# Pinning weight transfers, activation-sum transfers and a norm scaling to program order in the down stage

## The chip, the cores and the metric

The kernel is one program on one core of a Trainium2 chip. The metric is the device time of one execution in microseconds (us), and less is better. Before the change three runs took 1169.48, 1171.72 and 1176.24 us; the median is 1171.72 us. The profiled execution is a fourth one, with a time of its own.

## The reference, cut to what matters

One decoder layer over 16 meta tokens and 256 sequence tokens, model width 2048. Two groups of heads (differential attention and retention) share an input projection and an output projection; a gated MLP of width 5632 with a causal convolution over three tokens follows, and then a final RMS norm. Everything is float32.

```python
u = rmsnorm(h, attn_norm[l]) * vmask
proj = u @ w_in[l]
...
y = jnp.concatenate([ya.reshape(B, L, D_A), yr.reshape(B, L, D_R)], axis=-1)
h = h + y @ w_out[l]
u = rmsnorm(h, ffn_norm[l]) * vmask
h = h + conv_glu(u, w_gate[l], w_up[l], conv_w[l], w_down[l])
out = rmsnorm(h, final_norm)

def conv_glu(u, w_gate, w_up, conv_w, w_down):
    g = u @ w_gate
    gc = ...                      # three-tap causal convolution of g
    return (jax.nn.silu(gc) * (u @ w_up)) @ w_down
```

The change touches the last product, `@ w_down`, a 256 x 5632 by 5632 x 2048 product, and the multiplication by `final_norm` behind it.

## The kernel before, in words

**Splitting.** A float32 operand is carried as two parts, a rounded "hi" part and the remainder "lo", and a product is three matmuls: hi by hi, hi by lo and lo by hi. So each piece of weights that arrives in SBUF is prepared twice before TensorE can use it: ScalarE (ACT) casts it into a tile `whi` (L180), and VectorE (DVE) subtracts that from the original into `wlo` (L181). There are three `whi` and three `wlo` buffers, so a cast waits until TensorE has finished with the piece three places earlier.

**Stages.** Input projection and heads, output projection, gate and up products (44 blocks `f`, L740 on), then the down stage, which starts about 924 us into the span and ends with the output. Weights stream in from HBM as chunks of 128 x 2048 floats (1 MB), one DMA each (L162), issued by SyncE (SP) on one queue. A chunk goes into one of three buffers with the tag `raw`. SP issues in its order and waits, at each DMA, until that DMA's buffer is free; whatever stands behind it on SP waits too.

**The down stage.** Output columns are handled in two groups `g` of 1024. Of the 44 blocks of 128 MLP channels, the first 16 are multiplied in eight pairs by a scheme that needs seven block products where four 2 x 2 blocks would need eight. Its weights are the eight "mixed" chunks of a group (`in_w_mix_dram`), and it uses sums of activations as well as the activations. Those sums were made in the gate and up stage and stored in DRAM tiles `sd`; in the down stage they come back as eight transfers of 512 KB into the two tiles `sf` (L159). A mixed chunk is worked in four parts, `b`, `d`, `u` and `t`, each of which needs an addition or subtraction on DVE besides the cast and the `wlo` (L188 to L196). The other 28 blocks are plain chunks (`in_w_down_dram`), of which each gives two entries of twelve matmuls. `down_order` writes the sequence: in group 0, six plain entries lead, and then the parts of the mixed chunks and the rest of the plain entries alternate; group 1 begins with a mixed chunk.

**Buffers that matter here.** A mixed chunk of even number goes into a buffer of its own, `sraw` in the pool `dn`; the odd ones use `raw`. `dn` stands where the pool of the gate and up stage (`fw`) stood, so `sraw` is free only once the last gate and up block has been finished on DVE (L763, `flo`). The two `sf` tiles stand where the gate and up stage's input stood, and each is free once TensorE has read its half for the last time.

**The final norm's vector.** Half of it at a time is broadcast into the tile `fn` by a DMA that GpSimd (POOL) issues (L792, `norm`), and DVE multiplies it by -0.5 (L797, `norm_scale`). It is used by `weigh` (L836), after a group's sums have been added up. The program text puts `norm_scale` twelve empty steps of the side list behind `norm`.

**What sets the order.** The kernel is written as one stream of instructions. A scheduler that has a time model of its own then decides, for each engine, the order in which the instructions stand; it keeps dependencies, and not the order of the text. In the text, `load` issues a mixed chunk's `sf` transfer immediately ahead of the chunk itself. The call `tc.keep_in_program_order(ins)` adds an edge of order (no wait) from the instruction that stands before `ins` on the same engine in the text.

Of the kernel before, what the change touches and what calls it, by code (L numbers as in the profile page):

```python
# [10 lines left out]
F32 = mybir.dt.float32  # L11
# [4 lines left out]
ALU = mybir.AluOpType  # L16
# [67 lines left out]
def down_order():  # L84


    out = []
    for g in range(2):
        plain = [("w", 2 * g + j, b) for j in range(2) for b in range(NPL)]
        parts = [("s", p, q) for p in range(NS) for q in PARTS]  # L90
        lead, tail = LEAD[g]
        mid = plain[lead:len(plain) - tail]
        seq = plain[:lead]
        done = 0
        for i, part in enumerate(parts):
            seq.append(part)
            to = (i + 1) * len(mid) // len(parts)
            seq += mid[done:to]
            done = to
        out.append(seq + plain[len(plain) - tail:])  # L100
    return out
# [3 lines left out]
def trunk_kernel(ctx, tc, a, out):  # L105
    nc = tc.nc
    V, S, PE = nc.vector, nc.scalar, nc.tensor
# [10 lines left out]
    chunks = []  # L118
# [6 lines left out]
    for j in range(NF):  # L125
        chunks.append(a["w_gate"][j])
        chunks.append(a["w_up"][j])
    entries = [(c, h) for c in range(len(chunks)) for h in range(2)]
    order = down_order()
    mixed = {}  # L130
# [15 lines left out]
    pools = {}  # L146
# [5 lines left out]
    def load(c):  # L152
        if c in mixed and mixed[c] % 2 == 0:
            t = pools["dn"].tile([P, D], F32, tag="sraw", name=f"raw{c}")
        else:
            t = wp.tile([P, D], F32, tag="raw", bufs=3, name=f"raw{c}")
        if mixed.get(c, NS) < NS:
            p = mixed[c]
            nc.sync.dma_start(  # L159
                out=pools["sf"][p // (NS // 2)][:, p % (NS // 2)].rearrange(  # L160
                    "p a b c -> p (a b c)").bitcast(F32), in_=pools["sd"][p])
        nc.sync.dma_start(out=t, in_=chunks[c])  # L162
        raw[c] = t

    def prep(hf):
# [41 lines left out]
    def ahead(hf):  # L207
        while state["dma"] < len(chunks) and opens[state["dma"]] <= hf + 4:
            load(state["dma"])
            state["dma"] += 1  # L210
        while state["prep"] < len(entries) and state["prep"] <= hf + 2:
            prep(state["prep"])
            state["prep"] += 1
# [49 lines left out]
    with tc.tile_pool(name="start", bufs=2) as st:  # L263
        acc = st.tile([P, 4, T], F32, name="acc", bufs=1)
        xrs, rws = [], []
        for c in range(4):
# [6 lines left out]
            for b, e in cuts:  # L273
                lead = c == 0 and b == 0
                (nc.scalar if lead else nc.sync).dma_start(
                    out=xr[:, b:e], in_=a["x"][:, 4 * c + b:4 * c + e])
# [5 lines left out]
        for c in range(4):  # L282
            xr, rw = xrs[c], rws[c]
            for half in range(2):
                whi = wp.tile([P, 1024], F32R, tag="whi", bufs=3, name=f"whi{2 * c + half}")
                wlo = wp.tile([P, 1024], F32R, tag="wlo", bufs=3, name=f"wlo{2 * c + half}")
                for jj in range(2):
# [6 lines left out]
                                           op0=ALU.mult, op1=ALU.subtract)  # L294
# [9 lines left out]
                    for t, (t0, n) in enumerate(FN):  # L304
                        b = jj * 512 + t * P
# [131 lines left out]
    with ExitStack() as p1:  # L437
# [203 lines left out]
        for h in range(AH):  # L641
# [6 lines left out]
                                   op0=ALU.mult, op1=ALU.mult)  # L648
# [20 lines left out]
        for kind, r in RSEQ:  # L669
            if kind == "g":  # L670
                for c in range(2):
                    g = ap_.tile([P, TV], F32, tag=f"g{c}", name=f"rg{r}_{c}")[:, :NQ]
# [28 lines left out]
        for j in range(KT):  # L701
# [15 lines left out]
            for i in range(4):  # L717
                c = j * P + i * 32
                nc.sync.dma_start(
                    out=hd[:, c:c + 32].rearrange("(b t) f -> t b f", t=32),  # L720
                    in_=hb[i * 32:(i + 1) * 32].rearrange("t (b f) -> t b f", f=32))
# [9 lines left out]
    with ExitStack() as p2:  # L731
# [6 lines left out]
        sd = [dp.tile([P, 8 * P], F32, name=f"sd{p}") for p in range(NS)]  # L738
        us = {}
        for f in range(NF):  # L740
            if f in (8, 16):
# [3 lines left out]
            g = fw.tile([P, NQ], F32, tag="g", name=f"fg{f}")  # L745
            V.tensor_tensor(out=g, in0=ps[:, :NQ], in1=rstd2, op=ALU.mult)
            c = fw.tile([P, SEQ], F32, tag="c", name=f"fc{f}")
            V.tensor_scalar(out=c, in0=g[:, 0:SEQ], scalar1=cw[:, f, 0:1], scalar2=None,
                            op0=ALU.mult)
# [17 lines left out]
            elif f < KP:  # L767
                a1, a2 = us.pop(f - 1), u
                p = f // 2
# [18 lines left out]
        fns = {}  # L788
# [5 lines left out]
            fns[g] = t  # L794

        def norm_scale(g):
            V.tensor_scalar(out=fns[g], in0=fns[g], scalar1=-0.5, scalar2=None, op0=ALU.mult)  # L797

        norm(0)
        side.extend([nop] * 12 + [lambda: norm_scale(0)])  # L800
        so = sp.tile([P, 2, NB + 1], F32, name="so", bufs=1)
        pre = sp.tile([P, 2], F32, name="pre", bufs=1)
# [60 lines left out]
        for g in range(2):  # L863
# [93 lines left out]
            if not g:  # L957
                take(0, 1)()
                take(1, 1)()
                side.extend([finish(0, 1), finish(1, 1), lambda: norm(1)])  # L960
                side.extend([nop] * 12 + [lambda: norm_scale(1)])
                continue
# [94 lines left out]
def build(arrs):  # L1057
    import concourse.bacc as _bacc
    import concourse.tile as _tile
    from concourse import mybir as _mybir  # L1060

    nc = _bacc.Bacc("TRN2", target_bir_lowering=False, num_devices=1)
    arrays, args = {}, {}
    for name, v in arrs.items():
        arrays[f"in_{name}_dram"] = v
        args[name] = nc.dram_tensor(f"in_{name}_dram", v.shape, _mybir.dt.from_np(v.dtype),
                                    kind="ExternalInput").ap()
    o = nc.dram_tensor("out_0_dram", (SEQ, D), _mybir.dt.from_np(np.dtype("float32")),
                       kind="ExternalOutput").ap()
    with _tile.TileContext(nc, schedule_with_timeline_sim=True) as tc:  # L1070
        trunk_kernel(tc, args, o)
    return nc, arrays
# [8 lines left out]
```

## Time and profile before

| | |
|---|---|
| median of 3 runs | 1171.72 us |
| lowest and highest run | 1169.48, 1176.24 us |
| the profiled execution's own time | 1175.15 us |
| its span, first to last instruction | 1173.2 us |
| mean granted TensorE clock | 0.994 |
| TensorE (PE) busy | 1151.7 us, 98% of the span |
| DVE busy | 903.2 us, 77% |
| ACT busy | 590.7 us, 50% |
| mean DMA rate | 198 GB/s |

The profiled execution lies 3.4 us above the median and within the three runs. It has 2.0 us outside the span of its instructions. "Busy" for TensorE counts every matmul for its whole pipelined duration, so that neighbours overlap; how fast it gets on is better read from the number of matmuls in a stretch of time. In the rows, PEld is the loading of stationary operands, SPq is the queue of instructions of SP, and a row "A L1 <- B L2: total, times, longest" says that A's line 1 sat idle until B's line 2 ended.

### The profile page before, as it was taken

How to read it: one execution, taken by the hardware profiler on the slowest of the kernel's cores; microseconds unless marked ns; L12 is line 12 of the kernel's file. 1: busy time of each engine (PE TensorE's matmuls, PEld its weight loads, DVE VectorE, ACT ScalarE, POOL GpSimd, SP SyncE). 2: the span in 40 equal slices, each digit the busy share in tenths (PEclk: the TensorE clock that was granted, in tenths of full speed). 3: DMA queues.
4: the chain of work that ended last, by engine and by line, in shares of the span. 5: the costliest groups of instructions: out<-in, count | busy, mean ns of one | idle time of the engine just before them, and what ended most of it. 6: DMA issues, size and time to landing. Idle time of an engine off the chain costs nothing.

```text
span 1173.2 us, 20383 instructions
## 1 busy us (share of the span) xinstructions
PE 1151.7 (98%) x7991; PEld 1073.7 (92%) x7991; DVE 903.2 (77%) x1697; ACT 590.7 (50%) x980; POOL 8.6 (1%) x32
## 2 busy tenths in 40 slices
PE   8999999999999999999999999999999989999997
PEld 7999999999999999999999999999999868887886
DVE  7888887757677769778777777777777678898885
ACT  7566665533345544444444444444444345555553
POOL 0000000000000000000000000000000000000000
PEclk9999999999999999999999999999999989999999
DMA  8545546555648776656555555555555855555642
GB/s 302 200 163 160 175 149 195 167 170 161 190 166 251 240 229 246 216 211 232 200 197 207 195 191 180 183 191 197 184 180 184 306 210 185 215 203 206 214 180 108
DMA packets 78976, 232.82 MB, mean 198 GB/s; under 512 B 41635, under 2 KB 49227, under 8 KB 54049
## 3 DMA queue, kind: packets, MB, share of 16 engines
q1 hardware_dynamic: 77296, 226.15, 55.9%
q0 software_dynamic: 1440, 5.24, 1.2%
q8 instruction: 62, 1.02, 0.3%
q14 instruction: 34, 0.27, 0.1%
q10 hardware_dynamic: 144, 0.14, 0.1%
HBM read 220.76 MB, written 10.75 MB: 197 GB/s over the span
## 4 chain that ended last, share of the span: by engine, by line
PE 81%; issue 11%; DMA 5%; DVE 2%; SPq 1%; ACT 0%; POOL 0%; DVEq 0%; ACTq 0%; POOLq 0%
PE mm L432 14%; PE mm L421 10%; PE mm L419 10%; PE mm L420 9%; PE mm L434 7%; PE mm L412 7%; PE mm L411 7%; PE mm L413 6%; PE o L809 2%; PE o L810 2%; PE o L808 2%; DMA rvt<-rhv 1%; DMA raw<-in_w_first_dram 1%; DMA raw<-in_w_in_dram 1%; PE po L539 1%
## 5 line engine op out<-in xcount | busy, mean ns | idle before, releaser
L180 ACT CAST whi<-raw 128x1024 fp32r<-128x1024 f32 (+1 forms) x413 | 418.1, 1017 | 433.7 <-issue 88.9
L181 DVE TENSOR_TENSOR wlo<-raw,whi 128x1024 fp32r<-128x1024 f32 (+1 forms) x413 | 485.9, 1182 | 177.0 <-ACT whi L180 170.7
L432 PE MATMUL mm<-g,whi 128*128 128x512 f32 x704 | 249.1, 393 | 0.0
L411 PE MATMUL mm<-x,whi 128*128 128x272 f32 (+1 forms) x688 | 199.9, 291 | 0.0
L412 PE MATMUL mm<-x,whi 128*128 128x272 f32 (+1 forms) x688 | 199.4, 290 | 0.0
L413 PE MATMUL mm<-x,wlo 128*128 128x272 f32 (+1 forms) x688 | 198.1, 288 | 1.2 <-DVE wlo L181 1.2
L419 PE MATMUL mm<-g,whi 128*128 128x260 f32 x704 | 198.8, 282 | 0.0
L421 PE MATMUL mm<-g,wlo 128*128 128x258 f32 x704 | 198.4, 282 | 0.0
L420 PE MATMUL mm<-g,whi 128*128 128x256 f32 x704 | 195.2, 277 | 0.0
L434 PE MATMUL mm<-g,wlo 128*128 128x256 f32 x660 | 185.4, 281 | 0.0
L432 PEld LDWEIGHTS mm<-g,whi 128*128 128x128 f32 x704 | 132.3, 188 | 25.7
L420 PEld LDWEIGHTS mm<-g,whi 128*128 128x128 f32 x704 | 133.6, 190 | 1.9
L419 PEld LDWEIGHTS mm<-g,whi 128*128 128x128 f32 x704 | 132.2, 188 | 0.0
L421 PEld LDWEIGHTS mm<-g,wlo 128*128 128x128 f32 x704 | 132.1, 188 | 0.0
L413 PEld LDWEIGHTS mm<-x,wlo 128*128 128x128 f32 x688 | 130.5, 190 | 1.4 <-DVE wlo L181 1.4
L411 PEld LDWEIGHTS mm<-x,whi 128*128 128x128 f32 x688 | 130.5, 190 | 0.0
L412 PEld LDWEIGHTS mm<-x,whi 128*128 128x128 f32 x688 | 130.5, 190 | 0.0
L434 PEld LDWEIGHTS mm<-g,wlo 128*128 128x128 f32 x660 | 124.4, 188 | 0.0
L809 PE MATMUL o<-wlo,fhi 128*128 128x512 f32 x238 | 93.9, 394 | 1.6 <-DVE wlo L181 1.6
L810 PE MATMUL o<-whi,flo 128*128 128x512 f32 x238 | 93.1, 391 | 0.0
L808 PE MATMUL o<-whi,fhi 128*128 128x512 f32 x238 | 85.4, 393 | 0.0
L419 PE MATMUL mm<-ys,whi 128*128 128x260 f32 x256 | 71.9, 282 | 0.0
(279 smaller groups left out, 1553.6 us busy)
## 6 DMA issues: line engine op xcount, KB each, us to landing
raw<-in_w_in_dram SPq DMA_DIRECT2D x44, 1024.0 KB
raw<-in_w_gate_dram SPq DMA_DIRECT2D x44, 1024.0 KB
raw<-in_w_up_dram SPq DMA_DIRECT2D x44, 1024.0 KB
raw<-in_w_down_dram SPq DMA_DIRECT2D x28, 1024.0 KB
raw<-in_w_out_dram SPq DMA_DIRECT2D x16, 1024.0 KB
raw<-in_w_mix_dram SPq DMA_DIRECT2D x16, 1024.0 KB
sd<-sh POOLq DMA_DIRECT2D x8, 512.0 KB, 2.9
sf<-sd SPq DMA_DIRECT2D x8, 512.0 KB
```

The source lines that it names most:

```text
L180: S.copy(out=hi[:, b:e], in_=src)
L181: V.tensor_tensor(out=lo[:, b:e], in0=src, in1=hi[:, b:e].bitcast(F32), op=ALU.subtract)
L411: PE.matmul(ps[:, :n], wh, xh, start=(k == 0), stop=False)
L412: PE.matmul(ps[:, :n], wh, xl, start=False, stop=False)
L413: PE.matmul(ps[:, :n], wl, xh, start=False, stop=(k == KT - 1))
L419: PE.matmul(ps[:, :NQ + 2], wh, src.cols(k, GO - 2, GL), start=(k == 0), stop=False)
L420: PE.matmul(ps[:, 4:NQ + 2], wh, src.cols(k, GL, GW), start=False, stop=False)
L421: PE.matmul(ps[:, 2:NQ + 2], wl, src.hi(k), start=False, stop=(k == KT - 1))
L432: PE.matmul(ps, wh, src.cols(k, GO + 2, GW), start=(k == 0), stop=(k == KT - 1))
L434: PE.matmul(ps[:, :SEQ], wl, src.cols(k, GO + 2, GL), start=False, stop=False)
L809: PE.matmul(o, ah, wl, start=False, stop=False)
L810: PE.matmul(o, al, wh, start=False, stop=stop)
```

## The change

Three kinds of instructions are pinned to the program's order on their engines: the eight `sf` transfers, all weight transfers of the down stage (chunk numbers from `nw` on), both on SP, and the two `norm_scale` instructions on DVE. No instruction is added, removed or altered.

```diff
@@ -125,6 +125,8 @@
         chunks.append(a["w_up"][j])
+    nw = len(chunks)
+    keep = tc.keep_in_program_order
     entries = [(c, h) for c in range(len(chunks)) for h in range(2)]
@@ -156,10 +158,12 @@
         if mixed.get(c, NS) < NS:
             p = mixed[c]
-            nc.sync.dma_start(
+            keep(nc.sync.dma_start(
                 out=pools["sf"][p // (NS // 2)][:, p % (NS // 2)].rearrange(
-                    "p a b c -> p (a b c)").bitcast(F32), in_=pools["sd"][p])
-        nc.sync.dma_start(out=t, in_=chunks[c])
+                    "p a b c -> p (a b c)").bitcast(F32), in_=pools["sd"][p]))
+        ins = nc.sync.dma_start(out=t, in_=chunks[c])
+        if c >= nw:
+            keep(ins)
         raw[c] = t
@@ -794,7 +798,8 @@
         def norm_scale(g):
-            V.tensor_scalar(out=fns[g], in0=fns[g], scalar1=-0.5, scalar2=None, op0=ALU.mult)
+            keep(V.tensor_scalar(out=fns[g], in0=fns[g], scalar1=-0.5, scalar2=None,
+                                 op0=ALU.mult))
```

What this does to the order shows at three places. Lines of the changed kernel carry other numbers for the same code: L159 is now L161, L162 is L164, L181 is L185, L188 to L196 are L192 to L200, L797 is L801.

**First place, SP at the start of the down stage.** `raw_11217` is the third plain chunk, `raw_11251` the first mixed chunk (number 0, in `sraw`), `raw_11342` the second mixed chunk, `raw_11286` and `raw_11373` the plain chunks behind them. Before:

```order
L162 DMA raw_11217<-in_w_down_dram 128x2048
L159 DMA sf_11203<-sd_5837 128x1024
L159 DMA sf_11203<-sd_5838 128x1024
L159 DMA sf_11203<-sd_5839 128x1024
L159 DMA sf_11203<-sd_5840 128x1024
L162 DMA raw_11286<-in_w_down_dram 128x2048
L159 DMA sf_11204<-sd_5841 128x1024
L159 DMA sf_11204<-sd_5842 128x1024
L159 DMA sf_11204<-sd_5843 128x1024
L159 DMA sf_11204<-sd_5844 128x1024
L162 DMA raw_11342<-in_w_mix_dram 128x2048
L162 DMA raw_11251<-in_w_mix_dram 128x2048
```

With the change:

```order
L164 DMA raw_11217<-in_w_down_dram 128x2048
L161 DMA sf_11203<-sd_5837 128x1024
L164 DMA raw_11251<-in_w_mix_dram 128x2048
L164 DMA raw_11286<-in_w_down_dram 128x2048
L161 DMA sf_11203<-sd_5838 128x1024
L164 DMA raw_11342<-in_w_mix_dram 128x2048
L164 DMA raw_11373<-in_w_down_dram 128x2048
L161 DMA sf_11203<-sd_5839 128x1024
L164 DMA raw_11424<-in_w_mix_dram 128x2048
L164 DMA raw_11445<-in_w_down_dram 128x2048
L161 DMA sf_11203<-sd_5840 128x1024
L164 DMA raw_11511<-in_w_mix_dram 128x2048
```

The first mixed chunk had eight `sf` transfers, a plain chunk and the second mixed chunk between itself and `raw_11217`; now it has one `sf` transfer, and the other seven stand one by one ahead of the mixed chunks that use them.

**Second place, DVE in the second mixed chunk of group 1** (`raw_12125`; `raw_12157` is the plain chunk whose `wlo_12190` follows, and `raw_12207` the third mixed chunk). Before:

```order
L181 TENSOR_TENSOR wlo_12160<-raw_12125,whi_12159 128x512
L181 TENSOR_TENSOR wlo_12173<-raw_12125,whi_12172 128x1024
L193 TENSOR_TENSOR raw_12125<-raw_12125 128x512
L797 TENSOR_SCALAR fn_12145<-fn_12145 128x1024
L196 TENSOR_TENSOR raw_12125<-raw_12125 128x512
L181 TENSOR_TENSOR wlo_12190<-raw_12157,whi_12189 128x1024
```

With the change, at the same place:

```order
L185 TENSOR_TENSOR wlo_12160<-raw_12125,whi_12159 128x512
L185 TENSOR_TENSOR wlo_12173<-raw_12125,whi_12172 128x1024
L197 TENSOR_TENSOR raw_12125<-raw_12125 128x512
L200 TENSOR_TENSOR raw_12125<-raw_12125 128x512
L185 TENSOR_TENSOR wlo_12190<-raw_12157,whi_12189 128x1024
```

and where the scaling went, one mixed chunk later:

```order
L200 TENSOR_TENSOR raw_12207<-raw_12207 128x512
L185 TENSOR_TENSOR wlo_12296<-raw_12225,whi_12295 128x1024
L185 TENSOR_TENSOR wlo_12308<-raw_12207,whi_12307 128x512
L185 TENSOR_TENSOR wlo_12308<-t_178_12241,whi_12307 128x512
L801 TENSOR_SCALAR fn_12145<-fn_12145 128x1024
L192 TENSOR_TENSOR t_181_12338<-raw_12305 128x512
```

The scaling stands 17 rows later. That of group 0 moves in the same way, 15 rows later, out of the preparation of the first mixed chunk.

**Third place, SP at the change of groups** (`raw_12011` is the first mixed chunk of group 1). Before:

```order
L162 DMA raw_11853<-in_w_mix_dram 128x2048
L162 DMA raw_11907<-in_w_down_dram 128x2048
L162 DMA raw_12011<-in_w_mix_dram 128x2048
L162 DMA raw_11944<-in_w_down_dram 128x2048
L162 DMA raw_11974<-in_w_down_dram 128x2048
L162 DMA raw_12054<-in_w_down_dram 128x2048
```

With the change:

```order
L164 DMA raw_11853<-in_w_mix_dram 128x2048
L164 DMA raw_11907<-in_w_down_dram 128x2048
L164 DMA raw_11944<-in_w_down_dram 128x2048
L164 DMA raw_11974<-in_w_down_dram 128x2048
L164 DMA raw_12011<-in_w_mix_dram 128x2048
L164 DMA raw_12054<-in_w_down_dram 128x2048
```

The mixed chunk goes two plain chunks later.

## The prediction

> **What bounds the kernel now.** I read the page, then the waits of the down stage, then windows around the longest of them, then the SP queue ahead of it. TensorE sets the time:
>
> ```profile
> PE 1151.7 (98%) x7991; PEld 1073.7 (92%) x7991; DVE 903.2 (77%) x1697; ACT 590.7 (50%) x980; POOL 8.6 (1%) x32
> ```
>
> The change touches only orders in the down stage, so it can win or lose only where TensorE idles or runs slowly there. The waits from 900 us to the end, longest rows that bear on it:
>
> ```profile
> ACT whi L180 <- DMA raw<-in_w_mix_dram: 10.9, 1, 10.9
> DVE t L188 <- DMA raw<-in_w_mix_dram: 9.7, 1, 9.7
> PE x L808 <- ACT whi L180: 4.6, 1, 4.6
> DVE fn L797 <- DMA fn<-in_final_norm_dram: 1.8, 1, 1.8
> PE o L809 <- DVE wlo L181: 1.6, 1, 1.6
> ```
>
> These hold the only two idle stretches of PE in that stretch of time, and each has its cause beside it: a mixed chunk that landed late, and a scaling on DVE that stood waiting for the norm's vector. In the windows the columns are the stretch, then busy time and count of PE, PEld, DVE, ACT and POOL, then the granted clock, the DMA share and GB/s:
>
> ```profile
> 930.50:940.90 10.40, 10.40 (x47) 8.39 (x45) 2.45 (x2) 1.83 (x2) 0.50 (x1) 1.00 1.00 404
> 940.90:945.60 4.70, 0.13 (x1) 0.00 (x0) 0.63 (x1) 0.65 (x2) 0.00 (x0) 0.92 0.96 406
> 945.60:951.70 6.10, 6.08 (x13) 4.21 (x14) 6.10 (x9) 3.76 (x5) 0.00 (x0) 0.50 0.03 11
> 956.00:1000.00 44.00, 44.00 (x195) 36.00 (x194) 38.51 (x46) 24.27 (x30) 0.00 (x0) 1.00 0.56 210
> ```
>
> The last row gives the undisturbed pace, 44.00 / 195 = 0.226 us a matmul. The row 945.60 says that the wait has a tail: half the clock for 6.1 us, in which 13 matmuls were done that need 13 x 0.226 = 2.9 us.
>
> **The first term: the first mixed chunk.** SP before:
>
> ```profile
> 921.92 1.75 SPq L159 DMA_DIRECT2D sf<-sd  x4
> 924.21 0.33 SPq L162 DMA_DIRECT2D raw<-in_w_down_dram  x1
> 924.71 2.21 SPq L159 DMA_DIRECT2D sf<-sd  x4
> 929.85 0.81 SPq L162 DMA_DIRECT2D raw<-in_w_mix_dram  x2
> 929.74 0.42 DVE L763 TENSOR_TENSOR flo<-ful,fhi 128x256 fp32r<-128x256 f32 x1
> 924.60:930.30 5.70, 5.70 (x27) 4.70 (x26) 3.97 (x6) 3.06 (x6) 0.00 (x0) 1.00 1.01 394
> ```
>
> The first mixed chunk is the second of the two issued from 929.85, so its issue is near 930.3. That instant does not move: its buffer is free when the last `flo` ends, 929.74 + 0.42 = 930.16. What moves is what lies ahead of it on the DMA engines. They are full (share 1.00) from 924.6 on: eight sums of 0.52 MB and two chunks of 1.05 MB stand ahead, and SP's own transfers are served in about that order, since the chunk was there only when ACT began, 944.95:
>
> ```profile
> 944.95 2.51 ACT L180 CAST whi<-raw 128x512 fp32r<-128x512 f32 x3 [10.94 <-DMA raw<-in_w_mix_dram]
> 953.34 0.33 SPq L162 DMA_DIRECT2D raw<-in_w_mix_dram  x1
> 953.40:954.40 1.00, 1.00 (x6) 0.84 (x5) 0.97 (x2) 0.10 (x1) 0.00 (x0) 1.00 0.46 66
> 954.40:957.60 3.20, 3.20 (x16) 2.66 (x15) 2.43 (x4) 2.62 (x3) 0.00 (x0) 1.00 0.80 310
> ```
>
> The last three rows are a mixed chunk that finds the engines free: issue at 953.34, then 0.07 + 3.2 x 0.310 = 1.06 MB, its whole size, by 957.6. That is 4.3 us, against 14.6 for the first one. With the change only one sum (issued at 921.9) is ahead of the first mixed chunk, and it has long landed by 930.3. So I expect the chunk by 930.3 + 4.3, with half a microsecond for the last engine: 935. A cast of 512 columns (a little over 0.6 us, 2.51 for two of them and a longer one) and two DVE steps of 0.69 make 936.5 for the first part. PE wants it here:
>
> ```profile
> 940.64 0.39 PE L810 MATMUL o<-whi,flo 128*128 128x512 f32 x1
> 945.62 0.79 PE L808 MATMUL x<-whi,fhi 128*128 128x512 f32 x1 [4.59 <-ACT whi L180]
> ```
>
> At pace it would start at 940.64 + 0.23 = 940.87, some 4 us after. Gain: 945.62 - 940.87 = 4.75, and the half clock, 6.10 - 2.9 = 3.2. **Term 1: 7.9 us.**
>
> What does the wait at SP's head now hold up? The plain chunk `raw_11286`, issued at 924.21 before, stands behind the mixed chunk and goes at about 930.7. It lands some 2.6 us behind it (1.05 MB at 404 GB/s), or 1.3 more where the norm's vector (0.52 MB) runs beside it: 939. Its cast needs the `whi` that PE frees at 940.9, so it still arrives in time. The seven other sums go one by one, 3.7 MB over the following 100 us, beside a DMA share of 0.56.
>
> **The half clock weighed.** In another place of this trace:
>
> ```profile
> 256.98 1.70 PE L596 MATMUL ro<-sd,rvt 86*128 86x172 f32 x10 [1.43 <-DMA rvt<-rhv]
> 258.80:262.20 3.40, 3.40 (x18) 3.40 (x17) 0.85 (x2) 0.98 (x3) 0.00 (x0) 0.50 0.08 34
> 1060.30:1062.70 2.40, 0.78 (x4) 0.34 (x3) 2.40 (x4) 0.87 (x1) 0.00 (x0) 1.00 0.48 201
> ```
>
> A wait of 1.4 us brought half clock for 3.4 us, and one of 1.6 us at 1060 none. So the tail of a wait is 3.4 or 6.1 us, or nothing, worth 1.7, 3.2 or 0. Another execution may pay a smaller tail than this one: term 1 is 6.5 to 7.9, and I take 7.9, the one seen here. [...]
>
> **The second term: the norm's scaling.**
>
> ```profile
> 1054.01 0.54 POOL L792 DMA_DIRECT2D fn<-in_final_norm_dram  x1 [123.01 <-DVE htok L836]
> 1057.71 0.69 DVE L193 TENSOR_TENSOR raw<-raw 128x512 f32<-128x512 f32 x1
> 1060.15 0.69 DVE L797 TENSOR_SCALAR fn<-fn 128x1024 f32<-128x1024 f32 x1 [1.75 <-DMA fn<-in_final_norm_dram]
> 1061.36 3.49 DVE L181 TENSOR_TENSOR wlo<-raw,whi 128x1024 fp32r<-128x1024 f32 x3
> 1058.22 2.95 ACT L180 CAST whi<-raw 128x1024 fp32r<-128x1024 f32 x3 [1.92 <-PE o L810]
> 1060.29 0.72 PE L808 MATMUL x<-whi,sf 128*128 128x512 f32 x2
> 1062.63 0.50 PE L809 MATMUL o<-wlo,fhi 128*128 128x512 f32 x1 [1.62 <-DVE wlo L181]
> ```
>
> DVE stood from 1058.4 to 1060.15 for a transfer issued at 1054.01, and PE then lacked a `wlo`. Moved 17 rows down, the scaling finds its data landed. Without it DVE takes L196 at 1058.4, and the `wlo` as the first cast ends (1058.22 + about 1 = 1059.2), so it ends at about 1060.5; PE wants it at 1060.29 + 2 x 0.226 = 1060.74. **Term 2:** 1062.63 - 1060.74 = **1.9 us**, with only 0.2 us to spare, so 1.4 to 1.9. The 0.69 us of the scaling itself stay on DVE, hidden behind matmuls at the new place; if that cover failed they would cost 0.7 once.
>
> **At no cost:** the first mixed chunk of group 1 goes two plain chunks later.
>
> ```profile
> 1020.06 0.33 SPq L162 DMA_DIRECT2D raw<-in_w_mix_dram  x1
> 1024.61 9.52 SPq L162 DMA_DIRECT2D raw<-in_w_down_dram  x3
> 1042.24 0.62 ACT L180 CAST whi<-raw 128x512 fp32r<-128x512 f32 x1 [1.09 <-issue]
> 1024.00:1045.00 21.00, 21.00 (x94) 17.14 (x93) 20.64 (x28) 11.66 (x17) 0.00 (x0) 1.00 0.59 210
> ```
>
> On the old clock it was issued at 1020.06; now it follows the second of the three plain chunks, at the latest with the third at 1033.8 (1024.61 + 9.52 - 0.33). It lands by 1033.8 + 4.8 = 1038.6, and its first cast is due at 1042.24. Should that fail, its two first DVE steps stand in a stretch where DVE is busy 20.64 of 21 us, so each microsecond over the 3.6 spare ones would cost PE one.
>
> **Sum:** 7.9 + 1.9 = 9.8 us, bounds 7.9 (6.5 + 1.4) to 9.8. Against the profiled execution that makes 1175.15 - 9.8 = 1165.3; it lay 3.4 us over the median, so against 1171.72 I forecast **1161.9 us**.
>
> **The rivals.**
> - *A shorter wait stays.* If the transfers in flight share the engines evenly, the first mixed chunk lands with its followers: two more chunks, a sum and the norm's vector, 4.2 MB in all, at 404 GB/s 10.4 us, from about 931.4: 941.8. PE then waits until its first part is ready, 942.4 to 943.2, about 2 us, and may pay a half clock of 1.7: gain 9.8 - 2 to 3.7, 1163.8 to 1165.6. For it speaks that the vector comes over another queue and does share; against it that in the profile the chunk came last, as it stood last.
> - *The pin does not bring the chunk earlier.* Its issue stays at 930.3; if the 14.6 us had another cause than what lay ahead (the buffer's place, for one), term 1 is lost, and 1.9 remains: 1169.8. Against it stands the same transfer in 4.3 us.
> - *Slower: the weight queue has no slack.* Seven sums now stand singly ahead of mixed chunks, 0.52 MB / 404 GB/s = 1.3 us each. It decides once a mixed chunk's slack falls under 1.3 us; then 7 x 1.3 = 9.1 are lost, and the chunk at the change of groups, at 14.6 us a transfer, lands at 1048.4, 6.2 late, with a tail of 3.2. Together 18.5 - 9.8: 1180.4. For it speaks DVE's full stretch; against it that the chunk issued at 953.34 ended at 957.6 and is first used at 964.15:
>
> ```profile
> 964.15 0.69 DVE L188 TENSOR_TENSOR t<-raw 128x512 f32<-128x512 f32 x1
> ```
>
> **How the numbers follow.** Forecast 0.76, shorter wait 0.14, no earlier chunk 0.06, slower 0.04. The forecast's own bounds are 1161.9 to 1163.8, and the runs before spread by 2 us below and 4.5 above their median, which a new median shares in part: 1158 below; above, the shorter wait's 1165.6 and some of that spread: 1168. Measurement tells 0.5%, 5.9 us, from no change: below 1165.9 counts as faster. The forecast falls there almost always, the shorter wait rather more often than not: 0.82. Within: the rest of the shorter wait and the case of 1169.8, 0.13. Slower: 0.05.
>
> **What would show it.** After the change the waits should have no PE row on `whi` L184 near the start of the down stage and none on `wlo` L185 behind the second `fn` transfer; the windows there should show clock 1.00 and 0.226 us a matmul; the ACT row for the first mixed chunk should wait for PE, not for a DMA, with hardly any DMA between 926 and 930. I am wrong if ACT still waits for `in_w_mix_dram` past 941, or if new PE waits appear behind `sf` or at the change of groups.

## The result, and the profile after

The changed kernel takes 1163.61 us (median of 11 runs, 1161.27 to 1167.64), the kernel before 1173.68 us in 11 runs (1169.48 to 1176.24). The ratio is 0.9921, 95% interval 0.9904 to 0.9938: 9.3 us faster, between 7.3 and 11.3 (the two medians differ by 10.1). The forecast was 1161.9 us and a gain of 9.8.

The profiled execution of the change has a span of 1162.7 us, 10.5 less than before. Not all of that belongs to the change. For the down stage, here are the first and the last kind of matmul in it, before and then with the change; the pair of times gives the start of the group's first and of its last instruction:

```profile
L808 PE MATMUL o<-whi,fhi x238: 388/389/629, 924.5 to 1154.9; 128*128 128x512 f32 x119
L810 PE MATMUL oe<-tailt,flo x8: 280/283/284, 1161.2 to 1165.0; 128*128 128x256 f32 x8
```

```profile
L813 PE MATMUL o<-whi,fhi x238: 388/389/497, 921.5 to 1144.3; 128*128 128x512 f32 x119
L815 PE MATMUL oe<-tailt,flo x8: 279/283/283, 1150.7 to 1154.5; 128*128 128x256 f32 x8
```

From first to last start the down stage took 1165.0 - 924.5 = 240.5 us before and 1154.5 - 921.5 = 233.0 us now: 7.5 us less. The other 3.0 us lie ahead of the down stage, where the engines go through the same order in both kernels, up to the sums' transfers on SP. Most of them can be seen: the profile of before has half clock from 258.80 to 262.20, which the prediction showed and put at 1.7 us, and its waits on `rvt` add up to 2.6 us against 1.6. In that part the profiles below differ by as much from each other (the down stage begins at 921 to 925 us in all of them but the last, which edits that part), so the 3.0 us are scatter between executions.

The first term of the prediction is seen directly. SP, ACT and DVE at the first mixed chunk, then windows (stretch, busy time and count of PE, PEld, DVE, ACT and POOL, granted clock, DMA share, GB/s):

```profile
927.27 0.33 SPq L164 DMA_DIRECT2D raw<-in_w_mix_dram  x1
932.66 0.62 ACT L184 CAST whi<-raw 128x512 fp32r<-128x512 f32 x1 [1.62 <-PE o L815]
932.21 0.69 DVE L192 TENSOR_TENSOR t<-raw 128x512 f32<-128x512 f32 x1
937.67 0.39 PE L815 MATMUL o<-whi,flo 128*128 128x512 f32 x1
937.90 0.39 PE L813 MATMUL x<-whi,fhi 128*128 128x512 f32 x1
```

```profile
922.50:927.00 4.50, 4.50 (x21) 3.73 (x20) 3.43 (x6) 2.24 (x4) 0.00 (x0) 1.00 0.00 0
927.30:932.30 5.00, 5.00 (x24) 4.14 (x23) 2.45 (x3) 2.06 (x2) 0.54 (x1) 1.00 0.78 276
937.90:942.70 4.80, 4.80 (x23) 3.98 (x22) 4.60 (x7) 3.15 (x4) 0.00 (x0) 1.00 0.99 417
942.70:948.70 6.00, 6.00 (x28) 4.99 (x27) 5.57 (x8) 2.92 (x4) 0.00 (x0) 1.00 0.87 300
```

The DMA engines are empty when the chunk is issued at 927.27, and DVE takes it at 932.21, at most 4.9 us later. The cast at 932.66 waits for TensorE to free a buffer, no longer for a DMA. TensorE goes from the last plain entry to the first mixed part in 0.23 us, and the clock stays at 1.00. For the second term, the scaling now runs without a wait, and there is none of PE at the old place:

```profile
1064.75 0.69 DVE L801 TENSOR_SCALAR fn<-fn 128x1024 f32<-128x1024 f32 x1
```

One thing is new in this profile, 220 us into the down stage. The waits in the stage, as sum, count and longest in us:

```profile
PE o L814 <- DVE wlo L185: 0.9, 1, 0.9
PE o L813 <- ACT whi L184: 0.2, 1, 0.2
ACT endt L184 <- DMA raw<-in_w_down_dram: 3.5, 1, 3.5
```

and the transfer behind them, in the chain of waits (start and time):

```profile
1126.32 8.77 DMA raw<-in_w_down_dram
```

A weight transfer near the end took 8.8 us from issue to landing, where the one in the prediction took 4.3. Whether the change causes that was the first question to the chip.

### The profile page after: what moved, and what is told of

The parts are those of the page before. It is cut to its first block, busy times and chain, and to the rows that moved or that the text cites. A ratio compares the mean times of both kernels' runs of the same rounds, so it can differ in the third digit from the quotient of the medians.

```text
span 1162.7 us, 20377 instructions
## 1 busy us (share of the span) xinstructions
PE 1147.3 (99%) x7991; PEld 1070.0 (92%) x7991; DVE 903.0 (78%) x1697; ACT 590.8 (51%) x980; POOL 8.6 (1%) x32
## 4 chain that ended last, share of the span: by engine, by line
PE 92%; DMA 4%; DVE 2%; ACT 1%; issue 1%; SPq 0%; DVEq 0%; ACTq 0%
PE mm L436 14%; PE mm L425 10%; PE mm L423 10%; PE mm L424 10%; PE mm L438 7%; PE mm L416 7%; PE mm L415 7%; PE mm L417 6%; PE o L814 5%; PE o L815 5%; PE o L813 5%; PE x L813 1%; DMA rvt<-rhv 1%; PE x L814 1%; PE x L815 1%; PE po L543 1%
## 5 line engine op out<-in xcount | busy, mean ns | idle before, releaser
L185 DVE TENSOR_TENSOR wlo<-raw,whi 128x1024 fp32r<-128x1024 f32 (+1 forms) x413 | 485.6, 1181 | 177.2 <-ACT whi L184 170.6
```

Source lines behind the costliest of these rows:

```text
L185: V.tensor_tensor(out=lo[:, b:e], in0=src, in1=hi[:, b:e].bitcast(F32), op=ALU.subtract)
```

## The experiments

All medians stand beside runs of the kernel before on the same chip. "Down stage" is always the difference between the two starts shown above, in the run's own profile.

### The change again

No edit: the changed kernel beside the partial versions.

> The changed kernel itself, run beside the partial versions below. My theory: 9.8 us faster than the kernel before, from a first term of 7.9 (4.75 us of wait for the first mixed chunk and 3.2 us of matmuls at half clock) and a second of 1.9 (a wait behind the norm's scaling). The profile of the change also showed a wait of 0.9 us on wlo and 0.2 us on whi some 220 us into the down stage, where one of 16 shares of a weight transfer landed about 3 us after the others. If that comes from the change, it shows here again at the same place; if it is an accident of one execution, it does not.

Measured: 1163.56 us, ratio 0.9911 (0.9887 to 0.9935). The down stage took 1153.5 - 922.4 = 231.1 us, 9.4 less than before, and PE has no wait in it at all. The first and last group of matmuls, then the wait of ACT that stands for the late weights:

```profile
L813 PE MATMUL o<-whi,fhi x238: 387/389/398, 922.4 to 1143.3; 128*128 128x512 f32 x119
L815 PE MATMUL oe<-tailt,flo x8: 279/283/283, 1149.6 to 1153.5; 128*128 128x256 f32 x8
```

```profile
ACT endt L184 <- DMA raw<-in_w_down_dram: 0.8, 1, 0.8
```

The late landing did not come back. A smaller one shows near the end of the version with the weights alone, below, and none in the other eight, where this wait is 0.7 to 1.7 us. Both cases have pinned weights, but SP's order near the end is the same in all versions, so two such cases cannot tell the pin from chance, and the cause stays open. It cost the first profile about the 1.9 us between 233.0 and 231.1, of which the two waits of TensorE shown there are 1.1. Without it the change gains 9.4 us in the down stage.

### The transfers alone

```diff
-            keep(V.tensor_scalar(out=fns[g], in0=fns[g], scalar1=-0.5, scalar2=None, ...))
+            V.tensor_scalar(out=fns[g], in0=fns[g], scalar1=-0.5, scalar2=None, ...)
```

> The pins on the transfers stay, those on the two scalings go. The scheduler now puts the first scaling ahead of the first mixed chunk's preparation on DVE, and the second in the second mixed chunk of group 1, much as before. Theory: the first term comes (7.9 us) less a new wait at the first mixed chunk, because the scaling waits for the norm's vector, which lands about 14.7 us into the down stage, and three DVE steps of 0.69 us then end at about 16.8 where TensorE wants the first wlo at 16.6 and the next at 17.5: 0.3 to 2 us. The second wait of 1.6 to 1.9 us stays. So 6 to 8 us faster. Rival, that the scalings carry the gain: about nothing.

Measured: 1166.64 us, ratio 0.9938 (0.9916 to 0.9959); down stage 233.9 us, 6.6 less than before. DVE at the first scaling, in the timeline, and then the waits on the vector and those of TensorE behind them:

```profile
936.35 0.69 DVE L801 TENSOR_SCALAR fn<-fn 128x1024 f32<-128x1024 f32 x1 [4.05 <-DMA fn<-in_final_norm_dram]
```

```profile
DVE fn L801 <- DMA fn<-in_final_norm_dram: 4.9, 2, 4.1
PE o L814 <- DVE wlo L185: 1.5, 2, 0.9
```

As expected, but for the second wait, which is 0.9 us here and not 1.6 to 1.9. With the weights early and the scaling free, the scheduler puts the scaling ahead of the first mixed chunk's preparation, and DVE then stands there for 4.05 us. The order before has no such stall at the first scaling, so its pin is needed only because the transfers are pinned.

### The scalings alone

```diff
-            keep(nc.sync.dma_start(
+            (nc.sync.dma_start(
                 out=pools["sf"][p // (NS // 2)][:, p % (NS // 2)].rearrange(...)...
-        if c >= nw:
+        if c >= len(chunks):
             keep(ins)
```

> The pins on the two scalings stay, those on the transfers go, and SP has the order of before. Theory: the second term alone, 1.9 us faster (0.16%), the wait for the first mixed chunk (about 4.6 us) and the half clock behind it are still in the profile. Rival, that the first stall came from the scaling in the middle of that chunk's preparation: about 8 us faster and no wait of 4.6 us.

Measured: 1170.47 us, ratio 0.9974 (0.9959 to 0.9989): 3.0 us faster, between 1.3 and 4.8; down stage 238.0 us, 2.5 less. The first wait is still there, a little shorter, and it is PE's only one in the stage:

```profile
PE x L813 <- ACT whi L184: 4.2, 1, 4.2
```

The rival, that the scaling in the middle of the preparation caused the first stall, falls. What the scaling is worth can be read from the starts of TensorE's matmuls. Behind the first stall this profile is 0.8 us further ahead of the one before than at the start of the stage, because the wait (4.2 us against 4.6) and the half clock were a little shorter in this execution. At the second scaling it gains 1.9 us, the forecast value, and 0.2 us go again before the end. Transfers alone and scalings alone give 6.6 + 2.5 = 9.1 of 9.4 us; that this comes so near is in part luck, since 0.8 of the 2.5 are not the scaling's and the transfers alone have a stall of their own.

### The sums alone

```diff
         ins = nc.sync.dma_start(out=t, in_=chunks[c])
-        if c >= nw:
+        if c >= len(chunks):
             keep(ins)
```

and the scalings unpinned as above.

> Only the eight transfers of activation sums are pinned; weights and scalings are not. On SP the second mixed chunk and a plain chunk still stand ahead of the first mixed chunk, and one sum instead of seven more. Theory (what lies ahead on the DMA engines decides): the first mixed chunk lands two chunks after 930, at about 937.5 on the clock of before, ahead of the 940.9 at which TensorE wants it, so the whole first term comes, 7.9 us, and the second wait of 1.9 stays. Rival (the pin on the weights is what matters): no gain or at most 3 us, with a wait for the mixed chunk left.

Measured: 1166.23 us, ratio 0.9934 (0.9914 to 0.9954); down stage 233.2 us, 7.3 less. The first mixed chunk still stands behind the second one, and its wait on `whi` is gone; two short ones on `wlo` are left:

```profile
ACT whi L184 <- DMA raw<-in_w_mix_dram: 4.5, 1, 4.5
PE o L814 <- DVE wlo L185: 2.0, 2, 1.3
```

ACT stands 4.5 us for the chunk, but that is the spare time: TensorE is still busy with the plain entries. Two sums are ahead of it here and not eight; the other six wait. So the backlog of sums was the cause, and not the chunk's own place.

### The sums and the scalings, weights free

Only the edit just shown; the scalings stay pinned.

> Sums and scalings pinned, weight transfers free: what the pin on the weights adds. On SP the second mixed chunk stands ahead of the first again. With the sums alone pinned, TensorE lost 0.9 us at the second part of the first mixed chunk (its wlo came late) and 1.4 us behind the norm's scaling. Theory: the scaling's loss goes, the 0.9 stays, and the first mixed chunk of group 1 goes out earlier without effect: about 9 us faster than before, 0.5 to 1 us slower than the full change. Rival (the pin on the weights is needed for the gain): at least 3 us slower than the full change.

Measured: 1164.51 us, ratio 0.9933 (0.9913 to 0.9953); down stage 231.3 us, 9.2 less, with no wait of PE. I had expected 0.9 us to stay at the first mixed chunk. About half of it went too, with the scaling that stood between the chunk's DVE steps: TensorE needs 3.6 us from the last plain matmul to the fourteenth behind it, and 3.2 in the profiles of the change. The pin on the weight transfers adds 0.2 us in the profile, which the runs can't tell from nothing.

### The weights alone

```diff
-            keep(nc.sync.dma_start(
+            (nc.sync.dma_start(
                 out=pools["sf"][p // (NS // 2)][:, p % (NS // 2)].rearrange(...)...
```

and the scalings unpinned; all weights of the down stage stay pinned.

> Only the weight transfers of the down stage are pinned; sums and scalings are free. The scheduler now puts all eight sums ahead of the third plain chunk on SP, and the first mixed chunk right behind that plain chunk. Theory: the eight sums (4.2 MB at about 0.4 MB/us) hold the DMA engines until about 933 on the clock of before, so the third plain chunk lands near 935 instead of 923 and TensorE waits for it by 1 to 3 us, at its ninth microsecond to eleventh in the down stage; the first mixed chunk then lands near 937.5, in time. So the stall moves to another chunk: 3 to 7 us faster than before, with a wait on whi or wlo of a plain chunk. Rival (pinning the weights suffices): 7.9 us faster and no new wait.

Measured: 1176.03 us, ratio 1.0021 (1.0001 to 1.0041): nothing gained and 2.5 us lost, between 0.1 and 4.8. The down stage took 1167.3 - 921.7 = 245.6 us in its profile, 5.1 more than before. I had the direction of the stall right and its price wrong by far. SP and ACT around the third plain chunk, then TensorE's waits, then the half clock behind the two longest:

```profile
919.06 4.64 SPq L161 DMA_DIRECT2D sf<-sd  x8
923.78 0.39 SPq L164 DMA_DIRECT2D raw<-in_w_down_dram  x1
936.86 1.99 ACT L184 CAST whi<-raw 128x1024 fp32r<-128x1024 f32 x2 [10.85 <-DMA raw<-in_w_down_dram]
```

```profile
PE o L813 <- ACT whi L184: 5.2, 1, 5.2
PE o L814 <- DVE wlo L185: 4.4, 2, 3.5
```

```profile
938.00:943.30 5.30, 5.26 (x12) 3.67 (x13) 5.30 (x7) 1.48 (x2) 0.00 (x0) 0.50 0.98 397
1062.80:1066.20 3.40, 3.40 (x10) 2.63 (x9) 1.37 (x2) 0.23 (x1) 0.00 (x0) 0.50 0.26 39
```

All eight sums now go ahead of the third plain chunk, which was issued at 923.78 and was there at 936.86, 13.1 us later. I had put its landing some 5 us earlier. I had counted the sums' bytes alone; the norm's vector beside them is 512 KB, 1.3 us at the 400 GB/s of these windows, and the rest of the 5 us I can't account for. TensorE waited 5.2 us with half clock behind it, and the wait on the scaling grew to 3.5 us, again with half clock. The other 0.9 us on `wlo` are the late weight near the end. Pinning one of two kinds of transfers moved the backlog ahead of a chunk that is wanted even earlier.

### A late first mixed chunk, in three sizes

The change, with one or two transfers more into the first mixed chunk's buffer ahead of the chunk:

```diff
+        if mixed.get(c) == 0:
+            keep(nc.sync.dma_start(out=t, in_=a["w_gate"][0]))
+            keep(nc.sync.dma_start(out=t[:, :512], in_=a["w_gate"][1][:, :512]))   # second size
         ins = nc.sync.dma_start(out=t, in_=chunks[c])
```

The first size has only the first extra line, and the third has a whole chunk in the second one too.

> The changed kernel with one more transfer of 1 MB (a chunk of other weights) into the first mixed chunk's buffer ahead of the chunk itself; the chunk waits for it. It lands about 4.6 us later, at about 15 us into the down stage, and TensorE wants its first part at 16.4. Theory: the spare time of some 4.5 us, which the change gives this chunk, just covers it: no wait at the first part or one under 1 us, perhaps as much at the plain chunk behind it; no half clock; within 2 us of the changed kernel. Rival (no spare time, the chunk is on the path): 4.6 us or more slower than the changed kernel.

> As before with one more transfer of a quarter of that size, also waited for: the first mixed chunk lands about 2.6 us later still, near 17.6 to 18.5 us into the down stage. Theory: TensorE waits 1.5 to 3 us. The question is the tail: the trace of before had half clock for 3.4 us after a wait of 1.4 us, and none after one of 1.6. Theory: a wait of this length may or may not bring it, 1.7 or 3.2 us if so. [...]

> Two extra transfers of 1 MB ahead of the first mixed chunk, each waited for: it lands some 9.3 us later than with the change, near 20 us into the down stage. Theory: TensorE waits about 4 to 5 us, as in the kernel before, and half clock follows for some 6.8 us, so that most of the first term (6 to 8 us of 7.9) is lost again and the kernel stands at 1170 to 1172 us. Rival (the wait before was due to the order of other work, not to the landing): no such wait.

Measured: 1165.31 us (ratio 0.9926, 0.9900 to 0.9952), 1169.06 us (0.9964, 0.9950 to 0.9978) and 1170.88 us (0.9985, 0.9968 to 1.0002). The down stages are 2.1, 5.6 and 7.0 us longer than the 231.1 of the change. One row of waits for each size, and behind that of the second and the third the windows with the half clock:

```profile
PE o L816 <- DVE wlo L187: 0.5, 1, 0.5
```

```profile
PE x L816 <- ACT whi L187: 3.1, 1, 3.1
```

```profile
941.80:945.20 3.40, 3.33 (x8) 2.15 (x8) 3.37 (x5) 2.11 (x3) 0.00 (x0) 0.50 1.04 436
945.20:952.00 6.80, 6.80 (x31) 5.63 (x31) 6.41 (x10) 3.86 (x5) 0.00 (x0) 1.00 1.00 378
```

```profile
PE x L816 <- ACT whi L187: 4.2, 1, 4.2
```

```profile
941.90:946.80 4.90, 4.80 (x11) 3.31 (x12) 4.87 (x8) 3.27 (x5) 0.00 (x0) 0.50 1.02 428
```

In the first size no wait is listed at the chunk's first matmul, so the change gives the first part about as much spare time as one such transfer takes (4.3 us in the prediction's rows, at most 4.9 in the first profile of the change), as expected. The parts behind it came late: the 2.1 us were all lost in this chunk, though the list puts only 0.7 down as waits of TensorE. In the second size the wait is a little longer than the 1.5 to 3 us expected, and the half clock came, which I had left open. With two whole transfers, the third size, the stall of the kernel before is back, wait and tail, by the landing alone, in the new order of everything else. That settles the first term's mechanism. A wait of 3.1 us was followed by 3.4 us of half clock, one of 4.2 by a longer stretch. By the matmuls done in these stretches (8 in 3.4 us and 11 in 4.9 us, at 0.226 us each for the full pace), the half clock was worth 1.6 and 2.4 us.

### One more empty step in the retention heads

The half clock behind short waits pointed at the retention stage, where TensorE waits twice in the profile of before (2.6 us in all, the longest 1.4) and in the second one of the change (2.4, 1.5). The change, with one more empty step of cover:

```diff
-            return [scores, vtr, nop, nop, nop, nop, nop, av, nop, stats, scale]
+            return [scores, vtr, nop, nop, nop, nop, nop, nop, av, nop, stats, scale]
```

> The changed kernel with one more empty step between the loading of the retention heads' values and their product, in an earlier stage (12 matmuls, 1.4 us, more cover). In the profiles TensorE waits there twice, 1.2 to 1.9 us each, 1.5 to 2.9 in all, and in two of them half clock followed for 3.4 us. Theory: those waits fall to some 0 to 1 us and the tails go, so 1 to 3 us faster than the change alone, about 10 to 12 us faster than before. Rival (the product then runs into something else, such as the statistics behind it): no gain.

Measured: 1160.46 us (1159.36 to 1161.25), ratio 0.9898 (0.9878 to 0.9919) to the kernel before. Its slowest run is about as fast as the fastest of the change in either job (1161.27 and 1161.55). The row of waits `PE ro L600 <- DMA rvt<-rhv`, which the change had with 2.4 us in its second profile, is gone; these two are the waits that PE has left ahead of the down stage, one at the very start of the kernel and one that all versions have:

```profile
PE psx L260 <- DVE warm L248: 1.7, 1, 1.7
PE mm L417 <- DVE wlo L185: 1.2, 1, 1.2
```

The down stage is unchanged at 231 us. This version is faster than both kernels. By the medians it is some 3 us below the change; measured against the kernel before beside each, it is 12.0 us faster where the change was 9.3 and 10.4, with intervals that overlap, so 2 to 3 us is what the runs support. Its profile also lacks two short waits in the first 50 us that the second profile of the change has (1.2 us together). They come ahead of the edited steps, so their absence is scatter and not a gain.

## Why the prediction was right

**Term 1, the first mixed chunk (forecast 7.9 us).** Its steps held one by one: the issue stayed behind `flo` (the chunk went out right after it), the engines were empty, the landing took at most 4.9 us where 4.8 was forecast, and the cast then waited for TensorE. That what lay ahead on the engines was the cause is shown from both sides: the sums alone brought the term without moving the chunk ahead of its neighbour, and extra transfers ahead of the chunk brought the stall back. By size, the starts of matmuls at the same place in TensorE's sequence show it, before and then with the change. The first pair lies behind the half clock, the second behind the wait on the scaling:

```profile
951.78 0.39 PE L809 MATMUL o<-wlo,fhi 128*128 128x512 f32 x1
940.84 0.39 PE L814 MATMUL o<-wlo,fhi 128*128 128x512 f32 x1
1063.21 0.39 PE L808 MATMUL o<-whi,fhi 128*128 128x512 f32 x1
1050.40 0.39 PE L813 MATMUL o<-whi,fhi 128*128 128x512 f32 x1
```

At the last plain matmul the change was 940.64 - 937.67 = 2.97 us ahead, at the first mixed one 945.62 - 937.90 = 7.72, and behind the half clock 10.94. So the wait gave 4.75 us and the half clock 3.2, together 8.0 where 7.9 was forecast. The second profile of the change gives the same 8.0.

**The half clock** as part of the stall's price is confirmed in four profiles: behind waits of 4.6, 5.2 and 4.2 us (before, the weights alone, the third size) the granted clock is 0.50, and behind the 4.2 us of the scalings alone there are matmuls of up to 628 ns where the median is 389, as in the profile of before (629). Its worth was rightly left as a bound: 2.4 us in the third size above, 3.2 in the profile of before.

**Term 2, the scaling (forecast 1.9).** From the first pair to the second the change gains another 12.81 - 10.94 = 1.9 us, and so does the version with the scalings alone. The 0.2 us that `wlo` had to spare were enough.

**At no cost.** The first mixed chunk of group 1, two plain chunks later, made no wait: PE has none at the change of groups in any version.

**The sum.** 9.8 was forecast. Behind the second term the profile had gained 12.81 - 2.97 = 9.8 us; 0.3 us were lost again later in the stage in both profiles of the change, for a reason that I did not find, which leaves the 9.4 of the second one. By the runs it is 9.3 (7.3 to 11.3). The median that the forecast started from, 1171.72 of three runs, was 1173.68 in eleven, which is where the 1.7 us between 1161.9 and 1163.6 come from.

**The rivals.** The shorter wait did not stay: no PE wait on the first mixed chunk in either profile of the change. The pin did bring the chunk earlier. The slower case, a queue without slack, did not come: in the first profile the DMA share rose from 0.56 to 0.62 over the 44 us that follow, and no `sf` or mixed chunk was waited for.

```profile
953.00:997.00 44.00, 44.00 (x194) 36.03 (x193) 38.87 (x47) 24.27 (x29) 0.00 (x0) 1.00 0.62 235
```

**What I did not see** is that the parts lean on each other. The prediction spoke of pins as if each kept its own term. In fact the weights' pin alone gains nothing, the transfers' pin alone makes the first scaling a new stall, and the sums' pin with the scalings' does all of it. Instructions that stay free can be placed anew by the scheduler once others are pinned. That holds for engines on which nothing was pinned too: from the first mixed chunk on, 24 places of TensorE's sequence hold another matmul than before, and ACT's order differs as well, which the three places shown ahead of the prediction leave out. No wait of TensorE comes from it.

## What to carry to other kernels

When a transfer lands late, look at what was issued ahead of it on the same engines and is wanted only later, before moving the transfer itself: here the sums ahead of the first mixed chunk cost 8 us, and holding back those that were wanted later brought most of it. An engine that works in its order should not be given a step that waits for a slow transfer among steps that feed the bottleneck (for the scaling DVE stood 1.75 us in the profile of before and 4.05 in the one with the transfers alone); the step can go wherever its data has surely landed. And a pin is a change to all that stays free: read the order that comes out on every engine, and pin what would otherwise move into the gap.

## What the runs showed of the hardware that I had not expected

The price of a TensorE wait was not proportional to its length. In these profiles waits of 4.2, 4.6 and 5.2 us (the third size, before, the weights alone) were followed by half clock for 4.9, 6.1 and 5.3 us, waits of 3.1 and 3.5 us by 3.4 us of it, and waits of 1.2 to 1.9 us sometimes by 3.4 us and sometimes by none: in the retention stage, the profile of the version with the sums alone has half clock behind a wait of 1.5 us at about 294 us,

```profile
297.40:300.90 3.50, 3.50 (x18) 3.50 (x18) 0.85 (x2) 0.80 (x3) 0.00 (x0) 0.51 0.07 30
```

and the second profile of the change, which has a wait of 1.5 us in the same stage, shows clock 1.00 from 255 to 262 us and from 296 to 302.

In the profile of before the two stretches of half clock within the kernel are 3.41 us (258.80 to 262.21) and 6.82 us (944.88 to 951.70) long; the longer one begins 0.7 us before the wait ends, at 945.62. The length of a wait alone does not say whether half clock follows: a wait of 1.9 us in the first size of the late chunk brought it (the first row), one of 1.8 us in the third size, which lies in the other two rows, brought none in them:

```profile
297.50:300.90 3.40, 3.40 (x15) 3.21 (x14) 0.43 (x1) 0.85 (x3) 0.00 (x0) 0.50 0.27 113
291.47:294.88 3.41, 2.28 (x18) 1.88 (x16) 2.16 (x3) 1.04 (x1) 0.00 (x0) 1.00 0.85 211
294.88:298.30 3.42, 2.73 (x20) 2.67 (x21) 0.95 (x2) 0.66 (x2) 0.00 (x0) 1.00 0.61 254
```

What separates the two is not shown by these runs.

In this kernel, whose TensorE is busy for 99% of the span of the change, taking away two waits of 2.4 us together went with 2 to 3 us less time, at a cost of one empty step; the second profile of the change had no half clock there, so in that profile it is the waits themselves, 2.4 us, that went.
